# All first parts of a weight unit, then all its second parts

## The chip, the cores and the metric

One core of a Trainium2 chip runs the whole program. The time is device microseconds of one execution. The profiled execution, from which all rows below come, took 1718.26 us; two timed executions took 1718.42 and 1718.72 us, median 1718.57 us.

## The reference, cut to what matters

The program computes two blocks of a network for 256 tokens of width 2048, in float32. The first block projects x with `w_in` into queries, keys, values and gates of eight attention heads, into four inputs of a short convolution and two of a pooling mixer; it mixes them, projects with `w_out` and normalises. The second block is a gated linear attention with four heads, a feed-forward layer (`silu(gate) * up`, 5632 wide) and a gated output. Nearly all of the arithmetic is products of the 256 tokens with weight matrices, and each weight is used once.

```
proj = jnp.einsum('bsd,de->bse', x, w_in[l])
...
gate, up = jnp.split(jnp.einsum('btd,de->bte', hn, w_in), 2, axis=-1)
return jnp.einsum('btf,fd->btd', jax.nn.silu(gate) * up, w_out)
```

## The kernel before, in words

Weights stream in as units of up to 128 x 2048 floats (1 MB). A class `Stream` holds the list of units and writes the order of the work out by hand. For each unit `_load` issues a DMA into a raw tile, `_hi` lets ScalarE round it into a first part `whi` (line 75), `_lo` lets VectorE (GpSimd for a few) subtract that from the raw tile to give a second part `wlo` (line 83), and then the unit's products run. Each of the three kinds of tile has three buffers, and the parts of unit w+2 are made in the step in which unit w runs: in the order H (first part), F, P (the work that follows the unit just finished), T, L (second part), or F, P, T, H, L where a unit is marked late. So the first part of unit w+2 goes into the buffer that unit w-1 has just left.

Activations are held in two parts too: `x[:, k, 0]` and `x[:, k, 1]`, 256 tokens each, side by side. A product of two such numbers is formed from three: first by first, first by second, second by first.

There are two kinds of products. In `tm_mm` (lines 202 to 204) the activations stand in the array and 512 columns of weights move past. In `fm_mm` (lines 171 to 183) the weights stand and tokens move: with `whi` standing, 512 columns move (both parts of x; a *wide* product, line 179), with `wlo` standing, 256 columns (the first part of x; a *narrow* product, lines 177 and 181). A unit of `fm_mm` has 16 slices kk, a wide and a narrow product each. With `zigzag` the order is hi0 lo0, lo1 hi1, lo2 hi2, ...; without it hi0 lo0, hi1 lo1, ... Every product has its own load of the standing operand (PEld in the profile).

The units of `fm_mm` are, in order: 24 of the attention heads (three per head), 16 of the convolution, 8 of the pooling mixer, 32 of the linear attention (eight per head: four for q and k, four for the output gate `og`), 48 of the first part of the feed-forward layer (f below `F_SPLIT`, line 1059 on) and 40 of its second part. The last 40 run without zigzag, all others with it. In every one of them the first part lies 16 elements into its padded tile (`SHIFT`), and the second part at the start of its own.

Each unit's sums are read by `join`: ScalarE copies the second 256 columns (line 187), VectorE adds the first 256 (line 188).

Two units do not have all of their activations when they start. The first unit of the linear attention (at 446 us in the profile) uses `hn`, whose last eight slices are made by `ln_hi` and `ln_lo` (lines 622 and 626) while it runs. The first unit of the feed-forward layer (at 886 us) has callbacks in the dictionary `mid`, which `fm_mm` calls after slices 1 and 4: they transpose the last four slices of `h` and make `hn[12]` to `hn[15]` of them (lines 981 and 982).

Of the kernel before, what the change touches and what calls it, by code (L numbers as in the profile page):

```python
# [17 lines left out]
P = 128  # L18
S = 256
# [4 lines left out]
PAD, SHIFT = 64, 16  # L24
# [14 lines left out]
class Stream:  # L39
# [29 lines left out]
    def _hi(self, w):  # L69
        if w < len(self.ws):  # L70
# [3 lines left out]
            hi = self.hi_p.tile([P, UN + PAD], F32R, tag="whi", name="whi")[:, self.ws[w][8]:]  # L74
# [3 lines left out]
    def _lo(self, w):  # L78
        if w < len(self.ws):
            n, eng = self.ws[w][1], self.ws[w][6]  # L80
            t, hi = self.raw.pop(w), self.parts[w][0]
            lo = self.lo_p.tile([P, UN + PAD], F32R, tag="wlo", name="wlo")
# [47 lines left out]
def program(ctx, tc, a, out):  # L130
# [40 lines left out]
    def fm_mm(ps, hi, lo, x, k0, n, first, last, m=P, zigzag=True):  # L171


        for kk in range(n):
            w, k = slice(kk * m, (kk + 1) * m), k0 + kk
            if kk and zigzag:
                MM(ps[:, :S], lhsT=lo[:, w], rhs=x[:, k, 0], start=False, stop=False)  # L177
            end = last and kk == n - 1
            MM(ps, lhsT=hi[:, w], rhs=x[:, k], start=first and kk == 0, stop=end and zigzag)  # L179
            if not kk or not zigzag:  # L180
                MM(ps[:, :S], lhsT=lo[:, w], rhs=x[:, k, 0], start=False, stop=end and not zigzag)  # L181
            for fn in mid.pop(kk, ()):
                fn()

# [21 lines left out]
    def fm_units(srcs, groups, xs, post, lo=None, late=False, zigzag=True):  # L206

        box = {}
        for j, (src, (k0, n)) in enumerate(zip(srcs, groups)):
            def mm(hi, lo, j=j, k0=k0, n=n):  # L210
                if j == 0:
                    box["ps"] = mmps()
                fm_mm(box["ps"], hi, lo, xs(), k0, n, j == 0, j == len(groups) - 1, zigzag=zigzag)

            st.unit(src, n * P, mm, (lambda: post(box["ps"])) if j == len(groups) - 1 else None, lo=lo, late=late, shift=SHIFT)

    def fm_unit(src, xs, post, lo=None, late=False, zigzag=True):
        fm_units([src], [(0, KT)], xs, post, lo, late, zigzag)
# [179 lines left out]
    for h in range(8):  # L398
# [56 lines left out]
        fm_unit(a["w1"][u0], xs, q_post)  # L455
        fm_unit(a["w1"][u0 + 1], xs, k_post)
        fm_unit(a["w1"][u0 + 2], xs, g_post)
        u0 += 3

    for c in range(4):  # L460
# [29 lines left out]
        for j, post in enumerate((cc_post, ch_post, cbb_post, cg_post)):  # L490
            fm_unit(a["w1"][u0 + j], xs, post)
        u0 += 4

    for g in range(4):
# [31 lines left out]
        fm_unit(a["w1"][u0], xs, pu_post)  # L526
        fm_unit(a["w1"][u0 + 1], xs, pg_post)
# [184 lines left out]
    def gla_head(h):  # L712
# [221 lines left out]
        def og():  # L934
            for j in range(4):
                fm_unit(a["w2"][h * 12 + 8 + j], hns, lambda ps, j=j: og_post(ps, j))
# [93 lines left out]
    def ffn_in(f, base):  # L1030
# [28 lines left out]
        fm_unit(a["ffn_in"][2 * f], hns, gate, zigzag=f < F_SPLIT)  # L1059
# [193 lines left out]
```

## Time and profile before

| what | value |
|---|---|
| profiled execution | 1718.26 us, its span 1716.5 us |
| median of two timed executions | 1718.57 us |
| TensorE | 1678.4 us busy, 98% of the span |
| weight loads (beside the products) | 1440.4 us, 84% |
| VectorE / ScalarE / GpSimd | 1073.8 / 796.7 / 76.9 us |
| DMA | 322.61 MB, 188 GB/s on average |
| granted TensorE clock | 0.994 of full speed |

A product's end in the profile is modelled and overlaps the next one, so what counts is the distance from one product's start to the next one's start. Where one line runs once in every unit, its first and last start and their count give the time of a unit.

### The profile page before, as it was taken

The page shows a single profiled execution, that of the slowest core. Times are in us where ns is not written, and L with a number is a line of the kernel's source. Part 1 is how long each engine was busy: PE and PEld are TensorE (multiplying, and loading weights), DVE is VectorE, ACT ScalarE, POOL GpSimd, SP SyncE. Part 2 cuts the span into 40 slices and gives each one's busy share as a digit, 9 for nine tenths or more (in the row PEclk, how much of TensorE's full clock was granted, in tenths as well). Part 3 has the DMA queues.
Part 4 walks back from the last instruction along what each step waited for, and adds up shares of the span by engine and source line. Part 5 has one row for each costly group of instructions (what it writes and reads, how often), then busy time and mean ns, then how long its engine had stood idle before and what let it go on. Part 6 is the DMA issues. An engine that isn't in the chain of part 4 may idle for free.

```text
span 1716.5 us, 21382 instructions
## 1 busy us (share of the span) xinstructions
PE 1678.4 (98%) x8890; PEld 1440.4 (84%) x8890; DVE 1073.8 (63%) x1242; ACT 796.7 (46%) x911; POOL 76.9 (4%) x67
## 2 busy tenths in 40 slices
PE   8999999999899999999999999999999999999997
PEld 6888888888687887888888888888888888888886
DVE  5565666755977678657556666664446666655554
ACT  5444544442665455444444444443334444444443
POOL 0400000000700000000000000000000000000011
PEclk9999999999899999999999999999999999999999
DMA  8554455476463334346555555555555555555643
GB/s 284 197 194 174 150 194 196 173 265 217 161 260 137 131 123 165 130 158 252 178 183 182 180 192 196 179 190 199 194 195 185 192 190 195 194 196 196 247 174 119
DMA packets 49345, 322.61 MB, mean 188 GB/s; under 512 B 5656, under 2 KB 5984, under 8 KB 12512
## 3 DMA queue, kind: packets, MB, share of 16 engines
q1 hardware_dynamic: 49248, 321.25, 53.4%
q8 instruction: 69, 1.13, 0.3%
q14 instruction: 28, 0.23, 0.0%
HBM read 314.86 MB, written 6.30 MB: 187 GB/s over the span
## 4 chain that ended last, share of the span: by engine, by line
PE 61%; DVE 6%; ACT 2%; issue 1%; ACTq 0%; POOLq 0%; POOL 0%; DVEq 0%
PE mm L179 21%; PE mm L202 9%; PE mm L204 9%; PE mm L203 9%; PE mm L177 6%; PE mm L181 5%; DVE wlo L83 2%; DVE kq L850 1%; PE ax L829 1%; PE mm L883 1%; ACT km L853 0%; DVE tl L798 0%; PE ax L974 0%; ACT whi L75 0%; DVE at L838 0%
## 5 line engine op out<-in xcount | busy, mean ns | idle before, releaser
L75 ACT CAST whi<-raw 128x2048 fp32r<-128x2048 f32 (+1 forms) x292 | 546.7, 1872 | 606.4 <-PE mm L204 300.8
L83 DVE TENSOR_TENSOR wlo<-raw,whi 128x2048 fp32r<-128x2048 f32 (+1 forms) x290 | 661.9, 2283 | 207.5 <-ACT whi L75 207.2
L179 PE MATMUL mm<-hn,whi 128*128 128x512 f32 x1920 | 667.5, 394 | 1.2 <-ACT vh L872 0.7
L179 PEld LDWEIGHTS mm<-hn,whi 128*128 128x128 f32 x1920 | 358.3, 189 | 75.0 <-ACT vh L872 1.1
L177 PE MATMUL mm<-hn,wlo 128*128 128x256 f32 x1200 | 337.5, 281 | 0.0
L179 PE MATMUL mm<-xa,whi 128*128 128x512 f32 x768 | 268.7, 396 | 0.0
L177 PEld LDWEIGHTS mm<-hn,wlo 128*128 128x128 f32 x1200 | 227.9, 190 | 3.9 <-ACT hn L981 0.3
L181 PE MATMUL mm<-hn,wlo 128*128 128x256 f32 x720 | 199.5, 277 | 4.8 <-DVE wlo L83 4.8
L177 PE MATMUL mm<-xa,wlo 128*128 128x256 f32 x720 | 200.9, 279 | 0.0
L179 PEld LDWEIGHTS mm<-xa,whi 128*128 128x128 f32 x768 | 142.4, 188 | 27.9
L181 PEld LDWEIGHTS mm<-hn,wlo 128*128 128x128 f32 x720 | 135.4, 188 | 7.5 <-DVE wlo L83 5.3
L177 PEld LDWEIGHTS mm<-xa,wlo 128*128 128x128 f32 x720 | 135.9, 189 | 2.1
L202 PE MATMUL mm<-whi,g 128*128 128x512 f32 x352 | 137.3, 390 | 0.0
L204 PE MATMUL mm<-whi,g 128*128 128x512 f32 x352 | 137.0, 389 | 0.0
L203 PE MATMUL mm<-wlo,g 128*128 128x512 f32 x352 | 137.0, 389 | 0.0
L202 PE MATMUL mm<-whi,hn 128*128 128x512 f32 x256 | 101.3, 396 | 2.1 <-DVE og L188 2.1
L203 PE MATMUL mm<-wlo,hn 128*128 128x512 f32 x256 | 100.0, 390 | 0.0
L204 PE MATMUL mm<-whi,hn 128*128 128x512 f32 x256 | 99.9, 390 | 0.0
L204 PEld LDWEIGHTS mm<-whi,g 128*128 128x128 f32 x352 | 66.1, 188 | 13.8
L202 PEld LDWEIGHTS mm<-whi,g 128*128 128x128 f32 x352 | 66.1, 188 | 13.6
L203 PEld LDWEIGHTS mm<-wlo,g 128*128 128x128 f32 x352 | 66.1, 188 | 13.5
L188 DVE TENSOR_TENSOR fu<-mm,fu 128x256 f32<-128x256 f32 x44 | 18.7, 425 | 63.7 <-ACT fu L187 63.7
(259 smaller groups left out, 1757.8 us busy)
## 6 DMA issues: line engine op xcount, KB each, us to landing
raw<-in_w SPq DMA_DIRECT2D x100, 1024.0 KB, 4.8
raw<-in_ffn_in SPq DMA_DIRECT2D x88, 1024.0 KB, 4.9
raw<-in_ffn_out SPq DMA_DIRECT2D x44, 1024.0 KB, 4.9
raw<-in_w_out SPq DMA_DIRECT2D x16, 1024.0 KB, 5.0
raw<-in_gla_out SPq DMA_DIRECT2D x16, 1024.0 KB, 4.9
raw<-in_ple_gate SPq DMA_DIRECT2D x16, 1024.0 KB, 5.0
raw<-in_w SPq DMA_DIRECT2D x8, 512.0 KB, 5.8
xT<-in_xT SPq DMA_DIRECT2D x8, 256.0 KB, 6.0
```

Source lines behind the costliest of these rows:

```text
L75: self.nc.scalar.copy(hi[:, :n], self.raw[w][:, :n])
L83: eng.tensor_tensor(lo[:, :n], t[:, :n], hi[:, :n], op=ALU.subtract)
L177: MM(ps[:, :S], lhsT=lo[:, w], rhs=x[:, k, 0], start=False, stop=False)
L179: MM(ps, lhsT=hi[:, w], rhs=x[:, k], start=first and kk == 0, stop=end and zigzag)
L181: MM(ps[:, :S], lhsT=lo[:, w], rhs=x[:, k, 0], start=False, stop=end and not zigzag)
L188: V.tensor_tensor(dst, ps[:, :S], dst, op=ALU.add)
L202: MM(ps2[t], lhsT=x[:, k0 + kk, 0, tok], rhs=hi[:, w], start=b, stop=False)
L203: MM(ps2[t], lhsT=x[:, k0 + kk, 0, tok], rhs=lo[:, w], start=False, stop=False)
L204: MM(ps2[t], lhsT=x[:, k0 + kk, 1, tok], rhs=hi[:, w], start=False, stop=e)
L829: MM(ps[:, tok], lhsT=km[:, d, tok], rhs=rhs, start=(d == 0), stop=(d == 1))
L850: V.tensor_tensor(o, o, f, op=ALU.mult)
L883: MM(ps[:, i * S:(i + 1) * S], lhsT=hb["v"][:, j, v], rhs=hb["at"][:, j, :], start=(j == 0), stop=(j == 1))
```

## The change

In `fm_mm` a unit's products are put in another order: all 16 wide products with the first part standing, and then all 16 narrow ones with the second part standing. The callbacks of `mid` stand in the loop over the wide products. The option `zigzag` goes.

A new option, `three`, is used for the 24 units of the convolution and the pooling mixer: slice by slice, but after the first slice the wide product is written as two of 256 columns, with the same part standing in both, so that a slice has three products of 256 columns.

The first part now lies at the start of its tile, and the second part lies at an offset in its own: one of eight (0, 16, 32, 48, 8, 24, 4, 40 elements), by head, group or stretch of the feed-forward layer; the q and k units of the linear attention keep offset 0.

```
@@ -21,7 +21,7 @@
 KT = D // P
 UN = 2048
 
-PAD, SHIFT = 64, 16
+PAD, SHIFTS = 64, (0, 16, 32, 48, 8, 24, 4, 40)
 ALPHA = 2.0 ** 0.25
 BIG = 3.0e38
 
@@ -71,7 +71,7 @@
             n, pre_split = self.ws[w][1], self.ws[w][5]
             if pre_split is not None:
                 pre_split()
-            hi = self.hi_p.tile([P, UN + PAD], F32R, tag="whi", name="whi")[:, self.ws[w][8]:]
+            hi = self.hi_p.tile([P, UN + PAD], F32R, tag="whi", name="whi")
             self.nc.scalar.copy(hi[:, :n], self.raw[w][:, :n])
             self.parts[w] = [hi]
 
@@ -79,7 +79,7 @@
         if w < len(self.ws):
             n, eng = self.ws[w][1], self.ws[w][6]
             t, hi = self.raw.pop(w), self.parts[w][0]
-            lo = self.lo_p.tile([P, UN + PAD], F32R, tag="wlo", name="wlo")
+            lo = self.lo_p.tile([P, UN + PAD], F32R, tag="wlo", name="wlo")[:, self.ws[w][8]:]
             eng.tensor_tensor(lo[:, :n], t[:, :n], hi[:, :n], op=ALU.subtract)
             self.parts[w].append(lo)
 
@@ -168,19 +168,27 @@
     mid = {}
 
 
-    def fm_mm(ps, hi, lo, x, k0, n, first, last, m=P, zigzag=True):
-
-
+    def fm_mm(ps, hi, lo, x, k0, n, first, last, m=P, three=False):
+
+
+
+        for kk in range(n if three else 0):
+            w, k, b, e = slice(kk * m, (kk + 1) * m), k0 + kk, first and kk == 0, last and kk == n - 1
+            if b:
+                MM(ps, lhsT=hi[:, w], rhs=x[:, k], start=True, stop=False)
+            else:
+                MM(ps[:, :S], lhsT=hi[:, w], rhs=x[:, k, 0], start=False, stop=False)
+                MM(ps[:, S:], lhsT=hi[:, w], rhs=x[:, k, 1], start=False, stop=False)
+            MM(ps[:, :S], lhsT=lo[:, w], rhs=x[:, k, 0], start=False, stop=e)
+        if three:
+            return
         for kk in range(n):
-            w, k = slice(kk * m, (kk + 1) * m), k0 + kk
-            if kk and zigzag:
-                MM(ps[:, :S], lhsT=lo[:, w], rhs=x[:, k, 0], start=False, stop=False)
-            end = last and kk == n - 1
-            MM(ps, lhsT=hi[:, w], rhs=x[:, k], start=first and kk == 0, stop=end and zigzag)
-            if not kk or not zigzag:
-                MM(ps[:, :S], lhsT=lo[:, w], rhs=x[:, k, 0], start=False, stop=end and not zigzag)
+            MM(ps, lhsT=hi[:, kk * m:(kk + 1) * m], rhs=x[:, k0 + kk], start=first and kk == 0, stop=False)
             for fn in mid.pop(kk, ()):
                 fn()
+        for kk in range(n):
+            MM(ps[:, :S], lhsT=lo[:, kk * m:(kk + 1) * m], rhs=x[:, k0 + kk, 0], start=False,
+               stop=last and kk == n - 1)
 
     def join(dst, ps):
 
@@ -203,19 +211,19 @@
                 MM(ps2[t], lhsT=x[:, k0 + kk, 0, tok], rhs=lo[:, w], start=False, stop=False)
                 MM(ps2[t], lhsT=x[:, k0 + kk, 1, tok], rhs=hi[:, w], start=False, stop=e)
 
-    def fm_units(srcs, groups, xs, post, lo=None, late=False, zigzag=True):
+    def fm_units(srcs, groups, xs, post, lo=None, late=False, shift=0, three=False):
 
         box = {}
         for j, (src, (k0, n)) in enumerate(zip(srcs, groups)):
             def mm(hi, lo, j=j, k0=k0, n=n):
                 if j == 0:
                     box["ps"] = mmps()
-                fm_mm(box["ps"], hi, lo, xs(), k0, n, j == 0, j == len(groups) - 1, zigzag=zigzag)
-
-            st.unit(src, n * P, mm, (lambda: post(box["ps"])) if j == len(groups) - 1 else None, lo=lo, late=late, shift=SHIFT)
-
-    def fm_unit(src, xs, post, lo=None, late=False, zigzag=True):
-        fm_units([src], [(0, KT)], xs, post, lo, late, zigzag)
+                fm_mm(box["ps"], hi, lo, xs(), k0, n, j == 0, j == len(groups) - 1, three=three)
+
+            st.unit(src, n * P, mm, (lambda: post(box["ps"])) if j == len(groups) - 1 else None, lo=lo, late=late, shift=shift)
+
+    def fm_unit(src, xs, post, lo=None, late=False, shift=0, three=False):
+        fm_units([src], [(0, KT)], xs, post, lo, late, shift, three)
 
     def tm_units(srcs, groups, xs, post, lo=()):
 
@@ -452,9 +460,9 @@
         def g_post(ps, hb=hb):
             hb["sg"] = silu2(tb["p"], ps)
 
-        fm_unit(a["w1"][u0], xs, q_post)
-        fm_unit(a["w1"][u0 + 1], xs, k_post)
-        fm_unit(a["w1"][u0 + 2], xs, g_post)
+        fm_unit(a["w1"][u0], xs, q_post, shift=SHIFTS[h // 2])
+        fm_unit(a["w1"][u0 + 1], xs, k_post, shift=SHIFTS[h // 2])
+        fm_unit(a["w1"][u0 + 2], xs, g_post, shift=SHIFTS[h // 2])
         u0 += 3
 
     for c in range(4):
@@ -488,7 +496,7 @@
             split(y, 8 + c, yf)
 
         for j, post in enumerate((cc_post, ch_post, cbb_post, cg_post)):
-            fm_unit(a["w1"][u0 + j], xs, post)
+            fm_unit(a["w1"][u0 + j], xs, post, shift=SHIFTS[c], three=True)
         u0 += 4
 
     for g in range(4):
@@ -523,8 +531,8 @@
         def pg_post(ps, gb=gb):
             gb["sg"] = silu2(tb["p"], ps)
 
-        fm_unit(a["w1"][u0], xs, pu_post)
-        fm_unit(a["w1"][u0 + 1], xs, pg_post)
+        fm_unit(a["w1"][u0], xs, pu_post, shift=SHIFTS[4 + g], three=True)
+        fm_unit(a["w1"][u0 + 1], xs, pg_post, shift=SHIFTS[4 + g], three=True)
         u0 += 2
 
 
@@ -933,7 +941,7 @@
 
         def og():
             for j in range(4):
-                fm_unit(a["w2"][h * 12 + 8 + j], hns, lambda ps, j=j: og_post(ps, j))
+                fm_unit(a["w2"][h * 12 + 8 + j], hns, lambda ps, j=j: og_post(ps, j), shift=SHIFTS[h])
 
         return qk, v, og
 
@@ -1056,8 +1064,8 @@
             V.scalar_tensor_tensor(u, b["g"], 0.5, u, op0=ALU.mult, op1=ALU.mult)
             split(fx["g"], f - base, u)
 
-        fm_unit(a["ffn_in"][2 * f], hns, gate, zigzag=f < F_SPLIT)
-        fm_unit(a["ffn_in"][2 * f + 1], hns, up, zigzag=f < F_SPLIT)
+        fm_unit(a["ffn_in"][2 * f], hns, gate, shift=SHIFTS[2 * f // 11])
+        fm_unit(a["ffn_in"][2 * f + 1], hns, up, shift=SHIFTS[(2 * f + 1) // 11])
 
     gs = lambda: fx["g"]
     for part, (f0, f1) in enumerate(((0, F_SPLIT), (F_SPLIT, F_ALL))):
```

## Rows read from the trace of the kernel before

**Rows 1.** The page: span, then busy time, share and instructions of each engine.
```profile
span 1716.5 us, 21382 instructions
...
PE 1678.4 (98%) x8890; PEld 1440.4 (84%) x8890; DVE 1073.8 (63%) x1242; ACT 796.7 (46%) x911; POOL 76.9 (4%) x67
```

**Rows 2.** Groups by line and shape, TensorE: busy us, mean ns, idle before and releaser.
```profile
L181 PE MATMUL mm<-hn,wlo 128*128 128x256 f32 x720 | 199.5, 277 | 4.8 <-DVE wlo L83 4.8
```

**Rows 3.** One line, L181, 894 to 1157 us: minimum/median/maximum ns, first and last start.
```profile
L181 PEld LDWEIGHTS mm<-hn,wlo x47: 187/188/192, 894.1 to 1151.7; 128*128 128x128 f32 x47
```

**Rows 4.** The same view of L181 from 228 to 300 us.
```profile
L181 PEld LDWEIGHTS mm<-xa,wlo x13: 187/188/188, 232.8 to 299.9; 128*128 128x128 f32 x13
```

**Rows 5.** The same view of L187 from 1290 to 1500 us.
```profile
L187 ACT COPY fu<-mm x19: 358/358/362, 1300.7 to 1496.5; 128x256 f32<-128x256 f32 x19
```

**Rows 6.** Timeline of TensorE, 564.7 to 567.5 us: start, duration, instruction; first and last of twelve.
```profile
564.71 0.39 PE L202 MATMUL mm<-whi,hn 128*128 128x512 f32 x1
...
567.21 0.39 PE L204 MATMUL mm<-whi,hn 128*128 128x512 f32 x1
```

**Rows 7.** Timeline of TensorE at 911 us.
```profile
911.38 0.28 PE L181 MATMUL mm<-hn,wlo 128*128 128x256 f32 x1
911.49 0.28 PE L177 MATMUL mm<-hn,wlo 128*128 128x256 f32 x1
911.61 0.39 PE L179 MATMUL mm<-hn,whi 128*128 128x512 f32 x1
```

**Rows 8.** Timeline of TensorE at 905 us.
```profile
905.32 0.62 PE L179 MATMUL mm<-hn,whi 128*128 128x512 f32 x2
905.78 0.28 PE L181 MATMUL mm<-hn,wlo 128*128 128x256 f32 x1
```

**Rows 9.** Timeline of TensorE at 77 us, behind a score product.
```profile
77.61 0.39 PE L179 MATMUL mm<-xa,whi 128*128 128x512 f32 x1
...
77.95 0.39 PE L179 MATMUL mm<-xa,whi 128*128 128x512 f32 x1
```

**Rows 10.** Timeline of TensorE, 446 to 461 us.
```profile
446.71 0.40 PE L179 MATMUL mm<-hn,whi 128*128 128x512 f32 x1
...
451.93 0.58 PE L181 MATMUL mm<-hn,wlo 128*128 128x256 f32 x1 [4.83 <-DVE wlo L83]
...
459.98 0.40 PE L179 MATMUL ax<-hn,ln_wlr 128*32 128x512 f32 x1
```

**Rows 11.** Timeline of VectorE, 442 to 460 us.
```profile
453.95 4.59 DVE L626 TENSOR_TENSOR hn<-ln_hm,hn 128x1024 fp32r<-128x1024 f32 x2 [0.26 <-ACT hn L622]
```

**Rows 12.** One tile, hn, from 440 to 470 us.
```profile
L626 DVE TENSOR_TENSOR hn<-ln_hm,hn x4: 1249/2341/3426, 442.9 to 455.1; 128x1024 fp32r<-128x1024 f32 x4
```

**Rows 13.** Stretches: busy us (count) of PE, PEld, DVE, ACT, POOL; granted clock; DMA.
```profile
452.00:456.40 4.40, 4.40 (x15) 3.82 (x16) 4.14 (x6) 3.53 (x3) 4.32 (x2) 0.50 0.74 199
...
456.40:461.00 4.60, 4.31 (x24) 3.21 (x24) 4.60 (x2) 4.48 (x9) 4.52 (x3) 1.00 0.39 151
```

**Rows 14.** Timeline of VectorE, 886 to 896 us.
```profile
888.52 2.29 DVE L83 TENSOR_TENSOR wlo<-raw,whi 128x2048 fp32r<-128x2048 f32 x1 [1.25 <-ACT whi L75]
...
893.17 0.48 DVE L982 SCALAR_TENSOR_TENSOR hn<-ax,small,hn 128x256 fp32r<-128x256 f32 x1 [0.54 <-ACT hn L981]
```

**Rows 15.** Timeline of TensorE, 891 to 894.5 us.
```profile
893.71 0.74 PE L179 MATMUL mm<-hn,whi 128*128 128x512 f32 x2
894.29 0.28 PE L181 MATMUL mm<-hn,wlo 128*128 128x256 f32 x1
```

**Rows 16.** Stretches from 465 to 797 us and from 894 to 1157 us.
```profile
465.00:797.00 332.00, 320.36 (x1803) 278.99 (x1801) 235.81 (x324) 171.92 (x212) 3.69 (x6) 0.99 0.47 167
...
894.00:1157.00 263.00, 263.00 (x1508) 231.30 (x1508) 172.84 (x215) 122.11 (x144) 0.69 (x1) 1.00 0.54 185
```

**Rows 17.** Timeline of ScalarE at 1320 us.
```profile
1320.62 1.91 ACT L75 CAST whi<-raw 128x2048 fp32r<-128x2048 f32 x1 [1.90 <-PE mm L179]
...
1322.43 0.36 ACT L187 COPY fu<-mm 128x256 f32<-128x256 f32 x1
```

## The prediction

> **What bounds the kernel now.** The page comes first: TensorE is busy for 98% of the span, no other engine for more than 63% [rows 1]. But a product's end is modelled, so a busy TensorE can still be a slow one; what counts is the distance between starts. I therefore read the pace of a unit stage by stage, then the waits. From 894 to 1157 us TensorE has no gap at all at the full clock [rows 16], and a unit there takes (1151.7 - 894.1)/46 = 5.600 us [rows 3]. In the convolution and pooling stage it takes (299.9 - 232.8)/12 = 5.592 us [rows 4]. The second part of the feed-forward layer, the one without zigzag, does the same products in (1496.5 - 1300.7)/36 = 5.439 us [rows 5]. So one kind of unit has two paces, 0.350 and 0.340 us for a wide and a narrow product together. In the attention stage both occur: behind a score product the pair is back at 77.95 - 77.61 = 0.34 us, with zigzag [rows 9]. The pace is thus not a property of the order within a slice alone; some relation between the products and the loads persists through a unit or a stage, and I can only bound what a new order does to it.
>
> Waits are few. VectorE's second part held up the first narrow product by 4.8 us in all, in one place [rows 2, 10]. From 465 to 797 us TensorE is without work for 332 - 320.4 = 11.6 us [rows 16].
>
> **What a unit costs in the new order.** A run of wide products is measured with weights moving: twelve starts from 564.71 to 567.21 us, 2.50/11 = 0.2273 us each [rows 6]. Two wide products of `fm_mm` in a row took 0.46/2 = 0.23 us [rows 8]; I take 0.2273, as the longer run, and keep 0.23 as the upper end. A run of narrow ones longer than two does not occur. Its lower end is what the best pair leaves, 0.3399 - 0.2273 = 0.1126 us [rows 5, 6], its upper end what the slow pair leaves, 0.350 - 0.2273 = 0.1227 us [rows 3, 6]. The nearest row is two narrow products in succession, (911.61 - 911.38)/2 = 0.115 us [rows 7], and I take that. A unit is then 16 x 0.2273 + 16 x 0.115 = 5.477 us, between 5.439 and 16 x (0.23 + 0.1227) = 5.643.
>
> A unit in threes has one wide and 1 + 15 x 3 = 46 narrow products: 0.227 + 46 x 0.115 = 5.517 us, between 5.407 and 0.23 + 46 x 0.1227 = 5.874.
>
> Each product has its load, 0.188 us long [rows 3], yet narrow products start 0.115 us apart [rows 7]: the load of the next one runs beside the present one and its predecessor's tail. The Trainium skill (TensorE: Matmul & The Clock Gate, Part 3, The mechanism: what overlaps and what doesn't) says that a load overlaps products in flight only where its row group differs; these loads fill all rows, so the rule would leave none of them hidden, and the trace disagrees, at 0.115 us per product. The Trainium skill (the same page, LDWEIGHTS) puts a load at its columns divided by 1.2 GHz; an estimate from that page is 128/1.2 = 107 ns, under every narrow pace here, which would speak for the lower end.
>
> The sum over units, new less old:
> - first feed-forward part, 48 units: 48 x (5.477 - 5.600) = -5.9 (-7.7 to +2.1);
> - second part, 40 units, already at the good pace: 40 x (5.477 - 5.439) = +1.5 (0 to +8.2);
> - threes, 24 units: 24 x (5.517 - 5.592) = -1.8 (-4.4 to +6.8);
> - 24 attention and 32 linear-attention units, which mix both paces, at their mean of 5.520: 56 x (5.477 - 5.520) = -2.4 (-4.5 to +6.9).
> Together -8.6 us, between -16.6 and +24.0.
>
> **Two places that get later.** *At 446 us* TensorE made one wide product and waited 5 us for the second part; the unit ended at 459.98 [rows 10]. The new order needs that part later, so this wait goes. But the next thing late is `hn`: VectorE's pieces for the last eight slices start at 453.95, the last at 455.1, and they last 1.25 and 3.43 us [rows 11, 12], so slices 8 to 11 can start at 455.2 and 12 to 15 at 458.54. Nothing moves on VectorE. Before, only three pairs and a half stood behind 458.54; now four wide and all 16 narrow products do: 0.91 + 1.84 = 2.75 us at the full clock, end at 461.3, 1.3 later. TensorE will have been without work from 446.71 + 8 x 0.227 = 448.5 to 455.2. After the stop of 5 us before, the granted clock was 0.50, the level of 1.2 GHz, from 452 to 456.4 us and then 1.00 [rows 13], so I expect half clock again. All 20 at half would be 5.5 us (+4.1); I take the four wide ones at half, 1.82 + 1.84 = 3.66, end at 462.2: **+2.2** (+1.3 to +4.1). The low-rank product follows on TensorE at once, with no slack.
>
> *At 886 us* the last of `hn` is ready at 893.17 + 0.48 = 893.65, and the last wide product starts at 893.71 [rows 14, 15]; before, the unit ended with it. The callbacks come earlier in the new order, but VectorE's pieces stand behind the second part of 888.52 to 890.81 [rows 14], which waits for ScalarE and not for TensorE; so 893.65 stays. Then 16 narrow products follow: **+1.8**.
>
> **Costed at nothing.** The first part's buffer is left 1.8 us before the unit ends, so ScalarE's rounding (1.91 us) and then the copy out of the sums come that much earlier [rows 17]. In the feed-forward and convolution stages nothing waits for them: TensorE's own work hides both, 263.0 of 263 us [rows 16]. In the linear attention it could shorten some of the 11.6 us; I count up to 3 of them as the lower end. The second part's buffer is left as late as before. VectorE's and ScalarE's instructions stay the same in number and size, with other offsets; SP's loads and GpSimd's work keep their order. 360 more products and loads (24 x 15) are in the sum.
>
> **Sum.** -8.6 + 2.2 + 1.8 = -4.6 on the profiled 1718.26 (span 1716.5 [rows 1] and 1.8 around it): 1713.7. The median of the two timed runs lies 0.3 above the profiled one, so I say **1714**. With all ends together: -16.6 - 3 + 3.1 = -16.5, or +24.0 + 5.9 = +29.9.
>
> **Rivals.**
> *Narrow products in a run drag.* In a run every load has only one narrow product to hide beside, where it had a wide one half of the time. For it: the rows at the slow pace are of units in which two wide or two narrow products follow each other at the boundary [rows 7, 8], and now all do; no row has an offset of 4, 8, 24 or 40 elements. With x for a narrow product, all 168 units take 529.2 + 3408x (144 x 16 + 24 x 46 = 3408 narrow products) against 929.7 now; with the 4.0 of the two places the change loses from x = 0.1163 on. At 0.120 it is +13, 1731; at 0.1227 with wide products at 0.23, +28, 1746; over 2% only above 0.126. Against it: narrow products sit at 0.113 beside wide ones for 196 us [rows 5].
> *All units clean.* Runs settle as those of `tm_mm` do [rows 6]: x = 0.1126, the sum -16.6 + 4.0 = -12.6, 1706. For it: the pace of rows 5 holds over 40 units.
> *Added loads are not hidden*: the threes bring 360 loads, each 0.188 us [rows 3]; end to end they are 68 us, 1782. Against it: loads of 0.188 in slots of 0.115 [rows 7]. (This is what the rule of the Trainium skill's page TensorE: Matmul & The Clock Gate, Part 3, would do here.)
> *The new waits are worse*: all 20 products at 446 us at half clock (+1.9 over the forecast) and the low-rank product behind them for another 4.4 us, as long as the half clock lasted before [rows 13], which costs half of that: +4.1 in all, 1718.
>
> **Chances.** Forecast (x from 0.1135 to 0.1163, -10 to 0) 46%; clean 22%; drag 26%, 4 of them beyond 2%; unhidden loads 1%; the new waits alone 5%. The range, 1703 to 1731, leaves out the drag above 0.120 (some 13%) and the unhidden loads. A measurement of this kernel tells about 2%, 34 us, from no change: faster 1%, same 94%, slower 5%.
>
> **What would show it.** Starts within the narrow run of a feed-forward unit: 0.115 apart, 0.113 (clean) or 0.118 and more (drag). Units at 5.48 us in both feed-forward parts, threes at 5.52. No wait for a second part at 446 us but one for `hn` of some 6.7 us, at half clock after it; the unit at 886 us 1.8 us longer. I am wrong if one of the offsets changes a unit by more than 0.2 us, or if the wide runs leave 0.227.

## The result: slower by one per cent

The changed kernel took 1736.12 us (median of 1735.57 and 1736.67) against 1718.57: ratio 1.0097, interval 1.0073 to 1.012. The prediction was 1714 us in a range of 1703 to 1731. The sign was wrong, and the time lies above the range. By the measure of 2% it is no change, which had been given 94%; by the interval it is slower. Over the experiments, executions of the kernel before fall in two groups, 1718.0 to 1719.3 and 1723.1 to 1724.2 us, so a single execution beside another says nothing below some 6 us, and paces are read from the traces instead.

The page of the profile after, the lines that answer to [rows 1]:

```profile
span 1734.9 us, 22001 instructions
...
PE 1695.3 (98%) x9250; PEld 1469.1 (85%) x9250; DVE 1074.2 (62%) x1242; ACT 803.9 (46%) x911; POOL 75.1 (4%) x67
```

The span grew by 18.4 us and TensorE's busy time by 16.9; the 360 added products are there (9250 for 8890). The other engines do what they did. Groups by line and shape on TensorE, the wide and the narrow products of the run order (busy us, mean ns, idle before and who ended it):

```profile
L186 PE MATMUL mm<-hn,whi 128*128 128x512 f32 x1920 | 466.8, 395 | 9.1 <-DVE hn L634 6.6 <-DVE hn L990 1.9 <-ACT vh L880 0.7
L190 PE MATMUL mm<-hn,wlo 128*128 128x256 f32 x1920 | 249.2, 283 | 0.0
```

No narrow product waits for a second part any more (4.8 us in [rows 2]); instead wide ones wait for `hn`, 6.6 us at the first place and 1.9 at the second. Waits thus changed little, and the loss has to be looked for in the pace.

Timeline of TensorE in the second feed-forward part, four runs, the last cut off by the window (start, duration, instruction):

```profile
1421.43 2.06 PE L190 MATMUL mm<-hn,wlo 128*128 128x256 f32 x16
1423.32 3.83 PE L186 MATMUL mm<-hn,whi 128*128 128x512 f32 x16
1427.00 2.06 PE L190 MATMUL mm<-hn,wlo 128*128 128x256 f32 x16
1428.89 3.38 PE L186 MATMUL mm<-hn,whi 128*128 128x512 f32 x14
```

Starts are what counts: 16 narrow products take 1423.32 - 1421.43 = 1.89 us, 0.118 each; 16 wide ones 3.68, 0.230 each. The forecast had 0.115 and 0.2273. The time of a unit by a copy that runs in every second unit of the feed-forward layer and in every fourth of the convolution (count, first and last start): the first feed-forward part, the second, the convolution in threes:

```profile
L195 ACT COPY fu<-mm x21: 362/373/373, 926.1 to 1148.5; 128x256 f32<-128x256 f32 x21
...
L195 ACT COPY fu<-mm x17: 372/373/374, 1312.5 to 1490.4; 128x256 f32<-128x256 f32 x17
...
L195 ACT COPY cu<-mm x3: 361/363/366, 243.4 to 288.9; 128x256 f32<-128x256 f32 x3
```

With 40, 32 and 8 units from the first start to the last: 222.4/40 = 5.560 us, 177.9/32 = 5.559 and 45.5/8 = 5.69, where [rows 3], [rows 5] and [rows 4] gave 5.600, 5.439 and 5.592. So both feed-forward parts run at one pace now, between the two old ones.

The account of the 18.4 us, unit by unit (means from a unit's first product to the next unit's):

| units | before | after | sum, us | forecast, us |
|---|---|---|---|---|
| attention, 24 | 5.600 | 5.654 | +1.3 | -1.0 |
| convolution and pooling in threes, 24 | 5.599 | 5.725 | +3.0 | -1.8 |
| linear attention but the first, 31 | 5.759 | 5.778 | +0.6 | -1.3 |
| first feed-forward part but the first, 47 | 5.592 | 5.563 | -1.4 | -5.9 |
| second part, 40 | 5.440 | 5.562 | +4.9 | +1.5 |
| unit at 446 us before | 13.27 | 15.29 | +2.0 | +2.2 |
| unit at 886 us before | 7.67 | 10.57 | +2.9 | +1.8 |
| all else | | | +5.1 | 0 |

"All else" is 0.4 before the first product, 1.2 in front of the unit at 446 us, 2.9 between the other units of the linear attention, and 0.6 spread over the rest. There are stretches at half the clock beside the 1.2 and the 2.9, below.

The first late place, timeline of TensorE (it answers to [rows 10]):

```profile
453.01 2.01 PE L186 MATMUL mm<-hn,whi 128*128 128x512 f32 x8
460.34 2.08 PE L186 MATMUL mm<-hn,whi 128*128 128x512 f32 x4 [5.32 <-DVE hn L634]
463.66 2.08 PE L186 MATMUL mm<-hn,whi 128*128 128x512 f32 x4 [1.24 <-DVE hn L634]
465.53 2.94 PE L190 MATMUL mm<-hn,wlo 128*128 128x256 f32 x16
468.31 2.00 PE L186 MATMUL ax<-hn,ln_wlr 128*32 128x512 f32 x8
```

Eight wide products, a stop of 5.3 us for `hn`, four, a stop, four, sixteen narrow ones: the order of events is the forecast one. The wide products behind the stop last 2.08 us in fours. Stretches of the trace (PE, PEld, DVE, ACT, POOL busy; granted clock; DMA):

```profile
457.30:467.50 10.20, 5.92 (x18) 4.62 (x19) 9.94 (x7) 9.35 (x14) 10.04 (x4) 0.50 0.51 154
...
658.70:662.10 3.40, 3.40 (x11) 2.82 (x12) 3.37 (x5) 1.08 (x1) 0.00 (x0) 0.50 0.12 51
737.20:740.60 3.40, 3.40 (x10) 2.65 (x9) 2.47 (x4) 0.80 (x2) 0.00 (x0) 0.50 0.55 227
904.40:907.80 3.40, 3.12 (x11) 2.39 (x11) 1.07 (x5) 3.22 (x6) 0.69 (x1) 0.50 0.64 265
```

The granted clock was 0.50, the level of 1.2 GHz, for 10.2 us here, where before it was so for 6.8 (449.6 to 456.4, of which [rows 13] show the end). Here it ended at 467.5, among the sixteen narrow products and 0.8 us before the low-rank product. Ahead of the unit, from 440.2 us, it was so for 6.8 where before it was for 3.4. There are also two stretches inside the linear attention, at 658.7 and 737.2 us, and one at the second late place, that the profile before does not have. That place, timeline of TensorE:

```profile
901.67 0.39 PE L186 MATMUL mm<-hn,whi 128*128 128x512 f32 x1
903.11 0.49 PE L186 MATMUL mm<-hn,whi 128*128 128x512 f32 x1 [1.05 <-DVE hn L990]
904.14 1.14 PE L186 MATMUL mm<-hn,whi 128*128 128x512 f32 x2 [0.53 <-DVE hn L990]
905.56 0.79 PE L186 MATMUL mm<-hn,whi 128*128 128x512 f32 x1 [0.28 <-DVE hn L990]
906.15 2.81 PE L190 MATMUL mm<-hn,wlo 128*128 128x256 f32 x16
908.80 1.55 PE L186 MATMUL mm<-hn,whi 128*128 128x512 f32 x6
```

The sixteen narrow products behind the last `hn` took 908.80 - 906.15 = 2.65 us and not 1.84: about the first two thirds of that ran in the stretch at half clock. In [rows 15] nothing was left at this point.

### The profile page after: what moved, and what is told of

The parts are those of the page before. It is cut to its first block, busy times and chain, and to the rows that moved or that the text cites. A ratio compares the mean times of both kernels' runs of the same rounds, so it can differ in the third digit from the quotient of the medians.

```text
span 1734.9 us, 22001 instructions
## 1 busy us (share of the span) xinstructions
PE 1695.3 (98%) x9250; PEld 1469.1 (85%) x9250; DVE 1074.2 (62%) x1242; ACT 803.9 (46%) x911; POOL 75.1 (4%) x67
## 4 chain that ended last, share of the span: by engine, by line
PE 62%; DVE 5%; ACT 2%; issue 1%; ACTq 0%; POOLq 0%; POOL 0%; DVEq 0%
PE mm L186 22%; PE mm L190 11%; PE mm L210 9%; PE mm L211 9%; PE mm L212 9%; DVE wlo L83 1%; PE ax L837 1%; PE mm L891 1%; DVE kq L858 1%; PE ax L982 0%; DVE tl L806 0%; ACT km L861 0%; ACT whi L75 0%; DVE at L846 0%; DVE te L802 0%
## 5 line engine op out<-in xcount | busy, mean ns | idle before, releaser
L186 PE MATMUL mm<-hn,whi 128*128 128x512 f32 x1920 | 466.8, 395 | 9.1 <-DVE hn L634 6.6
L186 PEld LDWEIGHTS mm<-hn,whi 128*128 128x128 f32 x1920 | 354.7, 189 | 82.0 <-DVE hn L634 7.7
L190 PEld LDWEIGHTS mm<-hn,wlo 128*128 128x128 f32 x1920 | 246.6, 190 | 9.7
L190 PE MATMUL mm<-hn,wlo 128*128 128x256 f32 x1920 | 249.2, 283 | 0.0
L182 PE MATMUL mm<-xa,wlo 128*128 128x256 f32 x384 | 107.9, 281 | 0.0
L180 PE MATMUL mm<-xa,whi 128*128 128x256 f32 x360 | 101.5, 282 | 0.0
L181 PE MATMUL mm<-xa,whi 128*128 128x256 f32 x360 | 101.4, 282 | 0.0
L186 PE MATMUL mm<-xa,whi 128*128 128x512 f32 x384 | 93.9, 397 | 0.0
L186 PEld LDWEIGHTS mm<-xa,whi 128*128 128x128 f32 x384 | 71.0, 188 | 14.4
L182 PEld LDWEIGHTS mm<-xa,wlo 128*128 128x128 f32 x384 | 73.1, 190 | 0.1
L180 PEld LDWEIGHTS mm<-xa,whi 128*128 128x128 f32 x360 | 67.9, 189 | 1.1
```

Source lines behind the costliest of these rows:

```text
L180: MM(ps[:, :S], lhsT=hi[:, w], rhs=x[:, k, 0], start=False, stop=False)
L181: MM(ps[:, S:], lhsT=hi[:, w], rhs=x[:, k, 1], start=False, stop=False)
L186: MM(ps, lhsT=hi[:, kk * m:(kk + 1) * m], rhs=x[:, k0 + kk], start=first and kk == 0, stop=False)
L190: MM(ps[:, :S], lhsT=lo[:, kk * m:(kk + 1) * m], rhs=x[:, k0 + kk, 0], start=False, stop=last and kk == n - 1)
```

## The experiments

The unit's two halves are called standing parts below: first part `whi`, second part `wlo`. "In turn" means wide, narrow, wide, narrow through the slices; "run order" is that of the change. Three explanations of the narrow products' 0.118 were tried: A, their load is too long to hide beside a product of 256 columns; B, what is read for the load and for the product gets in each other's way, which the offset of the standing parts would alter; C, many products in a row add to the same sums.

### e1_paired: the order back, all else kept

In the plain units each narrow product follows its wide one again; threes and offsets stay.

```
             MM(ps, lhsT=hi[:, kk * m:(kk + 1) * m], rhs=x[:, k0 + kk], start=first and kk == 0, stop=False)
-            for fn in mid.pop(kk, ()):
-                fn()
-        for kk in range(n):
             MM(ps[:, :S], lhsT=lo[:, kk * m:(kk + 1) * m], rhs=x[:, k0 + kk, 0], start=False,
                stop=last and kk == n - 1)
+            for fn in mid.pop(kk, ()):
+                fn()
```

> The changed kernel with only the order of the plain units undone: wide and narrow product of a slice side by side; threes and the eight offsets stay. Theory (runs of narrow products drag): feed-forward units go from 5.53-5.58 us to 5.44 in both parts, the two units with late activations lose their 2.0 and 2.9 us, the threes keep their 3.2 us; total near 1736.1 - 88 x 0.12 - 4.9 - 3 = 1717-1718. Rival (the offsets of the second part, or the first part lying at offset 0, are what costs): units stay at 5.53-5.58, only the two places come back, total near 1731.

Measured: 1732.67 us, ratio 1.0066 (1.0042 to 1.0089). The feed-forward parts, first and second:

```profile
L194 ACT COPY fu<-mm x20: 355/359/364, 933.9 to 1145.3; 128x256 f32<-128x256 f32 x20
...
L194 ACT COPY fu<-mm x17: 356/362/368, 1320.3 to 1499.1; 128x256 f32<-128x256 f32 x17
```

That is 211.4/38 = 5.563 and 178.8/32 = 5.588 us a unit. Taking the order back did not bring back 5.439: at the offsets of the change, products in turn are no faster than products in runs, and the expectation's rival, at 1731, came true. The offsets are thus a cause of their own; this run does not tell whether the first part at 0 or the eight offsets of the second part do it. This profile also has an event in front of the first late place, on VectorE, and beside it one on GpSimd:

```profile
437.86 11.98 DVE L606 TENSOR_SCALAR ln_z<-ln_z,ln_rs,ln_nm 128x512 f32<-128x512 f32 x8
...
442.14 9.92 POOL L640 TENSOR_TENSOR ln_z<-ln_z,ln_rows 128x1024 f32<-128x1024 f32 x4 [1.92 <-PE ax L616]
```

Eight normalisations took 11.98 us; in the profiles before and after the same eight take 7.90 and 7.88. One of them takes 0.53 us, and 2.6 us where it starts while an instruction of GpSimd runs: here the first and the last three, these beside the work of line 640, and in the profiles before and after the first and the last alone. The edit touches neither engine's instructions; which of the two comes first there makes this execution some 4 us longer, and the profiles of e8 to e11 have 11.97 to 11.99 us too.

### e2_no_three: the threes alone undone

```
-                fm_mm(box["ps"], hi, lo, xs(), k0, n, j == 0, j == len(groups) - 1, three=three)
+                fm_mm(box["ps"], hi, lo, xs(), k0, n, j == 0, j == len(groups) - 1, three=False)
```

> The changed kernel without the threes: the 24 convolution and pooling units get the same order as the others. Theory: a unit in threes takes about 5.72 us (24 of them are 3.2 us longer than before), one with a wide and a narrow run 5.57; total falls by 24 x 0.15 = 3.7 us to 1732.4. Rival (the 360 added products and loads are hidden, the stage is slow for another reason): no change, 1736.

Measured: 1734.35 us, ratio 1.0071 (1.0049 to 1.0092). The convolution's units in run order:

```profile
L195 ACT COPY cu<-mm x3: 373/374/376, 241.5 to 286.0; 128x256 f32<-128x256 f32 x3
```

44.5/8 = 5.56 us, for 5.69 in threes. With the pooling units (5.638 for 5.748) the threes cost 16 x 0.130 + 8 x 0.110 = 3.0 us against the run order, and 3.0 against the kernel before. The medians differ by 1.8, which agrees but by itself would not be told from nothing.

### e4_two_places: run order everywhere but in the two late units

A flag `pair`, set for the units at 446 and 886 us alone, puts their products in turn.

```
+            if pair:
+                MM(ps[:, :S], lhsT=lo[:, kk * m:(kk + 1) * m], rhs=x[:, k0 + kk, 0], start=False,
+                   stop=last and kk == n - 1)
...
-        for kk in range(n):
+        for kk in range(0 if pair else n):
```

> The changed kernel with the paired order in two units alone, the first of the linear attention and the first of the feed-forward layer, whose activations come late. Theory: these two places cost 2.0 and 2.9 us, half clock behind them included; total falls by about 5 us to 1731. Rival (the half clock behind the stops comes whatever stands there, and the wait only moves): no more than 1.5 us, 1734.6 or above.

Measured: 1728.31 us, ratio 1.0045 (1.003 to 1.006). From the start of the first late unit to the start of the next layer's projection this profile needs 0.1 us more than the one before, and the first feed-forward part is 1.2 shorter than before (1.5 longer in the change): 2.7 us for the second place. Two stretches:

```profile
904.40:907.80 3.40, 3.40 (x21) 3.00 (x21) 0.89 (x3) 2.00 (x5) 0.00 (x0) 1.00 0.82 270
...
470.00:802.00 332.00, 320.59 (x1806) 280.11 (x1805) 236.52 (x326) 173.03 (x213) 3.91 (x6) 0.99 0.47 168
```

The clock is 1.00 where the change had 0.50. By medians the two places cost 1736.12 - 1728.31 = 7.8 us, by ratios 0.0052 x 1718.6 = 8.9, both uncertain by some microseconds, and not the 4.0 forecast. For the first place the profiles of e2 and e3, which keep the run order in it, have a unit of 16.9 and 17.0 us, and up to the next layer's projection they lose 3.6 and 3.8 on the profile before; the profile after has a unit of 15.3 and loses 6.7, of which 1.2 lie in front of the unit. Stretches at half clock like those at 658.7 and 737.2 us are absent from the profiles of e2, e3, e8 and e11, which have the run order, and stand in those of e10 and e12 (650.5, 729.0 and 725.1 us), which do not, and of e7, which does: they are put down to the execution, and what the order itself costs there is 3.6 to 3.8 us. With the 2.7 of the second place that is some 6.4.

### e5_before_paired: the kernel before with all units in turn

```
-                fm_mm(box["ps"], hi, lo, xs(), k0, n, j == 0, j == len(groups) - 1, zigzag=zigzag)
+                fm_mm(box["ps"], hi, lo, xs(), k0, n, j == 0, j == len(groups) - 1, zigzag=False)
```

> The kernel before with the zigzag off in all units, so that all run as its last 40 did: offset 16 for the first part, wide and narrow product of a slice in turn. Theory (the slow pace starts where two products of one width follow each other, so a strict alternation stays at 5.44): 48 feed-forward units gain 0.16 us each, 24 convolution and pooling units 0.15, the others about 0.08; 1718.6 - 7.7 - 3.6 - 4 = 1703. Rival (the good pace belongs to the last stage, not to the order): 1718.

Measured: 1721.09 us, ratio 0.9992 (0.9975 to 1.001). The first and the second feed-forward part:

```profile
L187 ACT COPY fu<-mm x20: 360/360/360, 928.5 to 1141.3; 128x256 f32<-128x256 f32 x20
...
L187 ACT COPY fu<-mm x17: 362/362/367, 1316.1 to 1490.2; 128x256 f32<-128x256 f32 x17
```

212.8/38 = 5.600 and 174.1/32 = 5.441 us. The same instructions on tiles at the same offsets, in one execution, at two paces. One unit near the start of the first part did take 5.443, and all behind it 5.60. My reading until then, that products in turn always run at the good pace, fell: a stage keeps one of two paces. TensorE's instructions in the two parts are the same, so I take it that what ran before decides which; no run sets that alone.

### e3_halves: narrow products on two sets of sums

```
-            MM(ps[:, :S], lhsT=lo[:, kk * m:(kk + 1) * m], rhs=x[:, k0 + kk, 0], start=False,
+            MM(ps[:, kk % 2 * S:(kk % 2 + 1) * S], lhsT=lo[:, kk * m:(kk + 1) * m], rhs=x[:, k0 + kk, 0], start=False,
```

> The changed kernel with the narrow products of a run going by turns into the first and the second 256 sums (join adds the two, so the result is the same). Theory A (a load is longer than a narrow product) and theory B (the reads of a load and of the moving tokens hinder each other): narrow products stay 0.118-0.120 us apart, units 5.53-5.58. Theory C (two products in succession that add to the same sums wait for each other): 0.113 apart, feed-forward units at 5.45-5.48, total some 14 us lower, 1722.

Measured: 1734.7 us in one execution. One narrow run and the wide one behind it:

```profile
1425.15 2.06 PE L190 MATMUL mm<-hn,wlo 128*128 128x256 f32 x16
1427.04 3.84 PE L186 MATMUL mm<-hn,whi 128*128 128x512 f32 x16
```

1.89/16 = 0.118 again: C is out as it was put. Both sets of sums lie side by side in one tile; sums further apart were not tried.

### e6_half_load: half as many columns loaded for a narrow product

```
+            h = m // 2 if m == P and kk < n - 1 else m
-            MM(ps[:, :S], lhsT=lo[:, kk * m:(kk + 1) * m], rhs=x[:, k0 + kk, 0], start=False,
+            MM(ps[:h, :S], lhsT=lo[:, kk * m:kk * m + h], rhs=x[:, k0 + kk, 0], start=False,
```

> The changed kernel with only 64 columns standing in all but the last narrow product of a run; it leaves out the second half of the columns of these products. Theory A (a load of 128 columns takes 0.118 us or more, a narrow product 0.113): the load is halved, narrow products come 0.113 apart. Theory B (each load costs some 5 ns by the reads that meet, whatever its length): 0.117-0.118 stays. Theory C (sums): 0.118 stays.

Measured: 1728.43 us in one execution.

```profile
1424.98 2.04 PE L191 MATMUL mm<-hn,wlo 128*64 128x256 f32 x16
1426.86 3.82 PE L186 MATMUL mm<-hn,whi 128*128 128x512 f32 x16
...
923.66 1.99 PE L191 MATMUL mm<-hn,wlo 128*64 128x256 f32 x16
925.49 3.81 PE L186 MATMUL mm<-hn,whi 128*128 128x512 f32 x16
```

1.88/16 = 0.1175, a mean of 0.117 over the feed-forward layer: half the load, hardly a saving in most places. The last two lines, from earlier in that layer, show the exception, the second part at offset 0: 1.83/16 = 0.114, where the change has 0.1195. At offset 16 half the load is slower (0.119 for 0.1175), at the other six it saves 0.0003 to 0.0034. The length of the load thus matters much at one offset and little at most, and does not set the pace by itself.

### e7_half_tokens: half as many tokens through a narrow product

```
-            MM(ps[:, :S], lhsT=lo[:, kk * m:(kk + 1) * m], rhs=x[:, k0 + kk, 0], start=False,
+            MM(ps[:, :S // 2], lhsT=lo[:, kk * m:(kk + 1) * m], rhs=x[:, k0 + kk, 0, :S // 2], start=False,
```

> The changed kernel with 128 tokens instead of 256 in the narrow runs; it leaves out the second half of the tokens in these products. The product is then shorter than any load, and the spacing shows what a load in a run takes. Theory A: 0.118, as with 256 tokens, units of 5.53 unchanged. Theory B: the load's own time without a long product beside it, below 0.113, near 0.108. Theory C: about 0.06. (If 128 tokens move at a lower rate, over 0.12.)

Measured: 1724.27 us in one execution.

```profile
1427.94 1.90 PE L190 MATMUL mm<-hn,wlo 128*128 128x128 f32 x16
1429.68 1.60 PE L186 MATMUL mm<-hn,whi 128*128 128x512 f32 x6
```

1.74/16 = 0.109, but the starts are uneven: in the feed-forward layer the second product of a run comes 0.057 to 0.065 us behind the first, and the others 0.107 to 0.115 apart, median 0.112. So where a load follows a load, it takes 0.112. That is less than the 0.113 of the good pace, if by little: a load fits beside a narrow product, and explanation A as it was put, with a load of 0.118 or more, is out. The Trainium skill (TensorE: Matmul & The Clock Gate, Part 2, LDWEIGHTS) gives a load its columns over 1.2 GHz, 107 ns as an estimate for 128; this run has 112, 5% more.

### e8_runs_old_offsets: run order with the offsets of before

The first part lies 16 elements into its tile and the second at the start, in the q and k units too; no threes.

```
-PAD, SHIFTS = 64, (0, 16, 32, 48, 8, 24, 4, 40)
+PAD, SHIFTS = 64, (16,) * 8
...
-            hi = self.hi_p.tile([P, UN + PAD], F32R, tag="whi", name="whi")
+            hi = self.hi_p.tile([P, UN + PAD], F32R, tag="whi", name="whi")[:, self.ws[w][8]:]
...
-            lo = self.lo_p.tile([P, UN + PAD], F32R, tag="wlo", name="wlo")[:, self.ws[w][8]:]
+            lo = self.lo_p.tile([P, UN + PAD], F32R, tag="wlo", name="wlo")
...
```

> The new order in runs with the offsets of the kernel before (first part 16 elements in, second part at 0) and without threes: order alone. If the order makes the pace, units stay at 5.53-5.58, narrow 0.118-0.120, total as without threes, 1730-1734. If offset 16 of the first part made the good pace of 5.44, it comes back in the last 40 units, 5 us lower.

Measured: 1745.6 us in one execution, the kernel before 1723.6 beside it.

```profile
1423.77 2.06 PE L190 MATMUL mm<-hn,wlo 128*128 128x256 f32 x16
1425.67 3.90 PE L186 MATMUL mm<-hn,whi 128*128 128x512 f32 x16
1429.41 1.82 PE L190 MATMUL mm<-hn,wlo 128*128 128x256 f32 x14
```

Narrow 1.90/16 = 0.119, wide 3.74/16 = 0.234, a unit 5.64. The run order by itself is worse than the change as a whole; the new offsets gave some of it back, on the wide products.

### e9_sweep: in turn, the first part at eight offsets

The order of e1 and the tiles of e8, without threes; each stretch has another offset of the first part, and the q and k units keep 0.

```
-PAD, SHIFTS = 64, (0, 16, 32, 48, 8, 24, 4, 40)
+PAD, SHIFTS = 64, (16, 32, 48, 64, 8, 24, 4, 40)
...
```

> Wide and narrow product of a slice in turn in all units, no threes; the second part at 0 and the first part at eight offsets (16, 32, 48, 64, 8, 24, 4, 40 elements), laid over heads, groups and the feed-forward layer as the changed kernel does with the second part. If the offset alone sets the pace, each offset has its own, the same wherever it stands, and one of them gives 5.44 us a unit everywhere. If what ran before decides as well (at offset 16 the same instructions take 5.44 us in the last 40 units and 5.60 in the 47 before them), the pace of one offset differs between stages and changes at the fp32 products that break a run.

Measured: 1731.05 us in one execution, the kernel before 1718.7 beside it. Units at offset 32 and at offset 48, in the first feed-forward part:

```profile
L194 ACT COPY fu<-mm x5: 361/365/367, 965.2 to 1010.3; 128x256 f32<-128x256 f32 x5
...
L194 ACT COPY fu<-mm x6: 355/364/366, 1021.6 to 1076.0; 128x256 f32<-128x256 f32 x6
```

45.1/8 = 5.64 and 54.4/10 = 5.440 us. At the others a unit takes 5.600 (16), 5.650 (64), 5.617 (8), 5.547 (24), 5.600 (4) and 5.590 (40). Only 48 reaches the good pace, here and in its four convolution units. From stretch to stretch a unit thus differs by up to 0.21 us. Each offset stands in a place of its own here, so what ran before differs too; e12 changes the offset alone.

### e10_turn_48: in turn, the first part at 48 everywhere

Otherwise as e9, the q and k units shifted too.

```
-PAD, SHIFTS = 64, (0, 16, 32, 48, 8, 24, 4, 40)
+PAD, SHIFTS = 64, (48, 48, 48, 48, 48, 48, 48, 48)
...
```

> Wide and narrow product in turn in all 168 units, first part 48 elements into its tile, second part at 0, no threes. In the sweep 15 units at this offset ran at 5.44 us in two stages, reached within one unit. If offset and order together decide: 47 feed-forward units gain 0.15 us each on the kernel before, 24 convolution and pooling units 0.15, the others some 3 us together, the last 40 stay at 5.44: 1718.6 - 7.2 - 3.7 - 3 = 1704.5, or 5 us more where the kernel before also takes 1723. Rival (the pace of a stage depends on what ran before it): some stage stays at 5.6, 1708-1718.

Measured: 1718.38 us, ratio 0.999 (0.9978 to 1.0002). The two feed-forward parts:

```profile
L194 ACT COPY fu<-mm x20: 361/361/361, 927.6 to 1140.4; 128x256 f32<-128x256 f32 x20
...
L194 ACT COPY fu<-mm x17: 362/366/366, 1315.2 to 1489.3; 128x256 f32<-128x256 f32 x17
```

212.8/38 = 5.600 and 174.1/32 = 5.441. The convolution reached 5.440 as well, but the first part stayed at 5.600, where e9 had reached 5.440 within a unit after coming from another offset. Again one offset has two paces, and what differs is what ran before.

### e11_runs_48: run order, the first part at 48

Otherwise as e8.

```
-PAD, SHIFTS = 64, (0, 16, 32, 48, 8, 24, 4, 40)
+PAD, SHIFTS = 64, (48,) * 8
...
```

> The order of the change (all wide, then all narrow products) at the offsets at which the products in turn run at 5.44: first part at 48, second at 0; no threes. If runs of narrow products drag at any offset: narrow 0.117-0.120, units 5.53-5.63. If the bad pace is a matter of the offset: narrow 0.113, units 5.44-5.46.

Measured: 1739.05 us in one execution.

```profile
1423.96 2.08 PE L190 MATMUL mm<-hn,wlo 128*128 128x256 f32 x16
1425.88 3.82 PE L186 MATMUL mm<-hn,whi 128*128 128x512 f32 x16
1429.54 1.72 PE L190 MATMUL mm<-hn,wlo 128*128 128x256 f32 x13
```

Narrow 1.92/16 = 0.120, wide 3.66/16 = 0.229. At the offset that is best in turn, narrow products in a run are as slow as ever. With the change's eight and e8 that makes ten settings of the offsets, with means from 0.1173 to 0.1204 in the feed-forward layer.

### e12_before_48: the kernel before with one number changed

```
-PAD, SHIFT = 64, 16
+PAD, SHIFT = 64, 48
```

> The kernel before with offset 48 in place of 16, zigzag kept: the offset alone. If strict alternation is needed to hold the good pace (each zigzag unit begins and ends with two products of one width): units stay at 5.59-5.60 with zigzag, 1718. If the offset alone decides: 5.44-5.46 in all stages, 1704.

Measured: 1712.2 us, ratio 0.995 (0.9932 to 0.9967): faster than both kernels by its interval, though by less than 2%. Its first feed-forward part, with zigzag:

```profile
L187 ACT COPY fu<-mm x20: 355/365/365, 934.2 to 1142.2; 128x256 f32<-128x256 f32 x20
```

208.0/38 = 5.474 us, where [rows 3] had 5.600. Here the offset alone was changed. That stage is 5.4 us shorter and the first block 1.0; the linear attention gained nothing.

## Why the prediction was wrong

**The step that failed** is the price of a narrow product in a run: "The nearest row is two narrow products in succession, (911.61 - 911.38)/2 = 0.115 us [rows 7], and I take that." In runs of sixteen they take 0.117 to 0.120 at every offset that ran, 0.1186 on average in the feed-forward layer. The trace of the kernel before could have told it. A timeline prints times to 0.01 us, and the 47 such pairs of that stage have a mean of 0.116; and directly behind the pair of [rows 7] stand single ones:

```profile
911.84 0.28 PE L177 MATMUL mm<-hn,wlo 128*128 128x256 f32 x1
911.96 0.39 PE L179 MATMUL mm<-hn,whi 128*128 128x512 f32 x1
912.19 0.28 PE L177 MATMUL mm<-hn,wlo 128*128 128x256 f32 x1
```

That is 0.12 us for a narrow product and 0.23 for a wide one; over the 47 units from 894 to 1157 us, 705 of each have means of 0.1176 and 0.2320. So the slow pace is not 0.2273 + 0.1227, as the prediction split it, and its narrow products take nearly as long in turn as in a run. The prediction's own limit, from which on the change loses, was 0.1163.

The rest of the units' sum is the wide products: 0.2273 from the run of `tm_mm` [rows 6] held as the median, 0.227, but the mean is 0.229, near the end that was kept for the range. With 3408 narrow products, 0.0036 more each is 12.3 us; with 2328 wide ones, 0.0017 more is 4.0. Forecast for the units -8.6, measured +8.4: a gap of 17.0 of the 23.0 us between 1713.7 and the profiled 1736.7.

**By steps.** *Threes*: forecast -1.8, measured +3.0; they hold 46 narrow products each, so the same price. That 360 added loads are not hidden, the rival at 1782, is out: they cost 3 us in all, and not 68. The Trainium skill (TensorE: Matmul & The Clock Gate, Part 3, The mechanism: what overlaps and what doesn't), by which a load overlaps only where its row group differs, is contradicted by that and by e7, where full loads recur every 0.112 us. *First part*: -1.4 for -5.9. *Second part*: +4.9 for +1.5. The direction of both was right, since the change levels the two paces; the level was wrong. *Attention and linear attention*: +1.9 for -2.3. Their "mean of 5.520" is the midpoint of the two paces and stands in no row: before the change these units took 5.600 and 5.759 us, waits within them included, and after it 5.654 and 5.778.

*The first late place*: waits, their order and half clock behind the stop came as forecast, and the unit cost +2.0 for +2.2 in the first profile, but 3.6 and 3.7 in those of e2 and e3; the close hit is luck in part. The half clock went on through the late wide products into the narrow ones, as the rival on new waits had it, but not into the low-rank product. *The second*: 893.65 plus sixteen narrow products was right in form; +2.9 for +1.8, because they ran partly at half clock. Ahead of that TensorE had made single wide products with pauses between them, from 901.67 us on; the forecast had priced the sixteen at the full clock.

*Costed at nothing*: right for the waits. Wide products in the feed-forward layer wait for nothing but `hn`, narrow ones for nothing at all. The 3 us that linear attention might have gained did not come. Not right for the new offsets, which the sum has at nothing without a reason: with them the second feed-forward part took 5.588 us a unit in turn (e1), where it had 5.440, some 6 us over its 40 units. Among the eight offsets of the second part a unit differs by 0.05 us at most; with the first part moved it is 0.21 (e9), just over the 0.2 that the prediction named as a sign of being wrong.

*Left out*: the remaining 5.1 us. In e3, with the same paces and a span 2.0 shorter, the two stretches at half clock in the linear attention are absent, and so are the 2.9 us between its units, while the first late unit is 1.7 longer; so some 2 to 3 of these microseconds belong to the profiled execution. The rest was not traced to a step.

**The rival that came true** was the drag of narrow products, at 26%. Its own formula gives 529.2 + 3408 x 0.1186 - 929.7 + 4.0 = +7.7, 1726.0 us; the wide products' 4.0 and the late places' 0.9 add up to 1730.9, and with the 5.1 left out it is 1736.0, 0.7 short of the measured. Its reason, that in a run a load has only a narrow product to hide beside, is not shown: e6 and e7 speak against the load's length as the cause, and in turn at the slow pace narrow products are nearly as slow. Too little weight was put on it: for 0.115 spoke one pair [rows 7].

**What is shown, and what stays open.** Shown: in runs, narrow products take 0.117 to 0.120 at all ten settings of the offsets (the change, e8, e11); neither the load's length alone (e6, e7) nor adding to the same sums (e3) sets that; the offset of the first part alone changes the pace of the old order (e12), and one offset can have two paces (e5, e10). Against the old order at the same offsets, a unit in runs costs 0.04 and 0.19 us more in the two feed-forward parts at 16 (e8 against the kernel before), 0.12 and 0.13 at 48 (e11 against e12), and nothing at the offsets of the change (e1): the second part lost its good pace, and either half of the change is enough for that. Not shown: what it is that the narrow products meet, and what chooses between the two paces. B is what is left, by exclusion alone; that half a load helps at one offset and not at others (e6) fits it.

## What to carry to other kernels

Read a spacing as a mean over many starts, not from one pair printed to a hundredth of a microsecond: 0.115 and 0.1176 lie on two sides of the limit from which on this change loses. When a change makes a run of something that so far came in pairs, take the slow pace as the likely one until a run is seen. Before reordering products, sweep the offset of the standing operand within its tile; here one number gave 0.5% and the reordering, with its new offsets, lost 1%. Work that is moved behind a late operand can cost more than its own time: here sixteen narrow products behind a stop took 2.65 us and not 1.84, partly at half clock.

## What the runs showed of the hardware

- The same products from the same offsets ran at 5.441 and at 5.600 us a unit within one execution (e5, e10), each pace over 32 units and more.
- With the first part 32 elements into its tile a unit took 5.64 us, with 48 elements 5.440 (e9); from 16 to 48 elements, and nothing else changed, the first feed-forward part went from 5.600 to 5.474 (e12). The Trainium skill (TensorE: Matmul & The Clock Gate, Part 2, Step-by-step: what each phase is for) says that loading the next weights takes no read bandwidth from the running product; no run here measures that bandwidth, and whether the offset acts by way of the reads is not shown.
- The profiled execution of the change has a mean granted clock of 0.938 and the other timed one 0.991, at 1736.67 and 1735.57 us: a record somewhat under 1.00 outside the stretches at 0.50 came with no slower products (0.118 and 0.230 us, where e3 at a mean of 0.992 has 0.118 and 0.229).
- Eight normalisations on VectorE took 7.9 us in nine of the profiles and 11.97 to 11.99 in five (e1, e8 to e11), with the same code: one takes 0.53 us, and 2.6 where it starts while an instruction of GpSimd runs, and in the five that holds for four of them and not two.
